# Retention with 128 rows for the sample's operands, and one block of modulation loads for each group

## The chip, the cores and the metric

The kernel runs on one core of a Trainium2 chip. The metric is the device time of one execution in microseconds (us), and what is compared is the median of several runs. Five engines run side by side, each in its own order: TensorE (PE in the profile, its weight loads PEld), VectorE (DVE), ScalarE (ACT), GpSimd (POOL) and SyncE (SP), which here issues most DMAs. They wait for each other by semaphores.

## What is computed

One layer of a streaming encoder, for 256 prompt rows and 32 sample rows together (T = 288), with 2048 features. Both kinds of rows use the same weights. Cut to what matters here:

```python
mod = silu(c) @ ada_w + ada_b                      # c: one vector for prompt, one for samples
shift, scale, gate = split(mod, 3)
h = rms_norm(x, g_pre) * (1 + scale) + shift
b, cg, u, zc, q, k, v, zr, ma, mb = split(h @ w_in)
y_conv = b * causal_conv(cg * u) * silu(zc)
# 8 heads of retention, q and k rotated by position, 128 wide, v 256 wide
scores = (q @ k.T) * decay                         # within a block
o = scores @ v + q_dec * (q @ state)
new_state = blk_dec * state + (k * k_dec).T @ v
y_ret = head_rms(o) * silu(zr)
merged = sigmoid(ma) * (y_conv @ w_branch[0]) + sigmoid(mb) * (y_ret @ w_branch[1])
x = x + gate * rms_norm(merged @ w_out, g_post)
```

Results are the new rows and the new states of the convolution and of retention.

## The kernel before

Activations lie with features in the partitions and the 288 rows in the free dimension. Every projection is made with three matmuls for each 128 x 128 piece of weights: the weights are cut into a high part (ScalarE, `whi`, L126 and L282) and a low part (VectorE, `wlo`, L127 and L289), the activations too (`hh`, `hl`), and high x high, high x low and low x high are added up in PSUM. Each of these is a matmul with 128 rows, 128 columns of weights and 288 moving columns.

*The start (L223 to L464)* runs in an order written out by hand for TensorE, ScalarE, VectorE and SP. The features are taken in eight groups of two 128-row tiles. For each group, shift and scale come from four loads of the modulation weights: `modulate` (L296) takes one load with eight small matmuls (L306), which write strips of 32 partitions; after the fourth, `gather_mod` (L313, L316), `factors` and `new_h` make the group's new activations. Then `multiply` (L357) multiplies three weight tiles of the group (w0, w1, w2: q, k and half of v), 48 matmuls each (L374, L375, L378), into `firsts`. VectorE or ScalarE adds the sums (L381, L383). While a tile is multiplied, later tiles are cut; `usual` and `rare` (L355) say after which quarter. In most groups a cut runs a tile and a half ahead of its use. The list `loads` (L250 to L254) sets both the order in which SP fetches and the order in which TensorE takes the loads. SP keeps eight loads in front (L459), in nine buffers, and issues one when the buffer it goes into is free. With m0 to m3 for the four loads of the next group's modulation, the order was w0 m0 m1 w1 m2 m3 w2 in group 0, and m0 w0 m1 w1 m2 m3 w2 in groups 1 to 6. Group 7 has no such loads.

*Retention (L473 to L621)* is ordered by a scheduler. For each pair of heads q and k are rotated (L481), for each head the gate is projected (L512) and, from head 4 on, the values (L503). A generator, `attend` (L520), is run a step at a time beside these projections: `step` (L169) is called after every twelve matmuls of the projection. Its steps, divided by `yield`, were: the keys turned (L532), scaled and cut; the values turned (L545, L546) and cut; the scores of two prompt blocks and of the samples (L553, L554, L555), decayed and cut; the new states (L572 for the samples); the outputs (L582 to L586), their norm; and three steps later the outputs turned back (L604). Products of two cut operands are three matmuls each (`add_product`, L497, L499 to L501). The prompt's operands have 128 rows; the samples' were sliced to 32: 32 rows of `kd` and `v`, of `pr` and `v`, of `on`; the samples' scores had 32 columns of k as weights. The operands' tiles were taken new by each head.

*After that* come the projections of the branches and of the convolution, and *the output projection (L757 on)*, whose result is copied (L773) and turned in 128 x 128 pieces (L775) and 128 x 32 pieces (L776).

Of the kernel before, what the change touches and what calls it, by code (L numbers as in the profile page):

```python
# [10 lines left out]
F32 = mybir.dt.float32  # L11
F32R = mybir.dt.float32r
# [4 lines left out]
P = 128  # L17
# [89 lines left out]
def hybrid_step(ctx: ExitStack, tc, x_prompt, x_sample, c_prompt, c_sample, state_conv, state_ret,  # L107
# [115 lines left out]
    with ExitStack() as phase:  # L223
# [27 lines left out]
        for g in range(NG):  # L251
            m = [(True, g + 1, s) for s in range(NK // MOD)] if g + 1 < NG else []
            w = [(False, g, u) for u in range(NU)]
            loads += (w[:1] + m[:1] if g == 0 else m[:1] + w[:1]) + m[1:2] + w[1:2] + m[2:] + w[2:]  # L254
        raws, parts_of, mod_ps, state_of = {}, {}, {}, {}
# [217 lines left out]
    with tc.tile_pool(name="ret", bufs=2, reuse_waits="tile") as rp:  # L473
# [5 lines left out]
        A.dma_start(out=qdec, in_=qdec_t)  # L479

        def rotate(ps, out):  # L481
# [12 lines left out]
        def parts(shape, name):  # L494
            return [rp.tile(shape, F32R, name=name + p, bufs=PB[name]) for p in ("h", "l")]

# [23 lines left out]
        def attend(h, q, k, vt, zs):  # L520

            state = rp.tile([P, DV], F32, name="state", bufs=1)
            A.dma_start(out=state, in_=state_ret[0, 0, h])
# [6 lines left out]
            for g in range(3):  # L530
                n = rows_of[g]
                nc.tensor.transpose(out=pk[:n, g * P:(g + 1) * P], in_=k[:, g * P:g * P + n], identity=ident)  # L532
            kd = parts([P, 3, DK], "kd")
            for g in range(3):
# [4 lines left out]
                                       op0=ALU.mult, op1=ALU.subtract)  # L539
            yield  # L540

            va, vb = aux_tile(), aux_tile()
            for f in range(2):
                for g in range(2):
                    nc.tensor.transpose(out=va[:, g * DV + f * P:g * DV + (f + 1) * P], in_=vt[f][:, g * P:(g + 1) * P], identity=ident)  # L545
                nc.tensor.transpose(out=vb[:TS, f * P:(f + 1) * P], in_=vt[f][:, TP:T], identity=ident)  # L546
            v = parts([P, 3, DV], "v")
            split(va.rearrange("p (g e) -> p g e", g=2), v[0][:, 0:2, :], v[1][:, 0:2, :])
# [5 lines left out]
            nc.tensor.matmul(psc[:, TP:TP + P], k[:, P:TP], q[:, P:TP], start=True, stop=True)  # L554
            nc.tensor.matmul(psc[:TS, TP + P:DC], k[:, TP:T], q[:, TP:T], start=True, stop=True)  # L555
# [3 lines left out]
            pr2 = parts([P, DC], "pr")  # L559
            split(pr[:, :TP + P], pr2[0][:, :TP + P], pr2[1][:, :TP + P])  # L560
# [4 lines left out]
            split(qs, *qs2)  # L565
            yield

            every, few = slice(None), slice(0, TS)
            pst = aux_tile()
            for g in range(2):  # L570
                add_product(pst[:, 0:DV], kd, v, (every, g), (every, g), g == 0, g == 1)
            add_product(pst[:, DV:2 * DV], kd, v, (few, 2), (few, 2), True, True)  # L572
            ns = rp.tile([P, 2, DV], F32, name="ns", bufs=1)
# [11 lines left out]
            add_product(ps[:TS, 0:DV], qs2, state2, (every,), (every,), True, False)  # L585
            add_product(ps[:TS, 0:DV], pr2, v, (few, slice(TP + P, DC)), (few, 2), False, True)  # L586
            so = rp.tile([P, 3], F32, name="so")
            V.memset(so, 1.0)
            on = rp.tile([P, 3, DV], F32, name="on", bufs=1)
            src = (po[:, 0:DV], po[:, DV:2 * DV], ps[:TS, 0:DV])  # L590
# [9 lines left out]
            for f in range(2):  # L600
                py = aux_tile()
                for g in range(3):
                    n = rows_of[g]
                    nc.tensor.transpose(out=py[:, g * P:g * P + n], in_=on[:n, g, f * P:(f + 1) * P], identity=ident[:n, :n])  # L604
                y = rp.tile([P, T], F32, name="y")
# [3 lines left out]
        for hp in range(NH // 2):  # L609
            qr, kr = turned(0, hp), turned(1, hp)  # L610
            for f in range(2):
                h = 2 * hp + f
                v = values(h)
                zs = gates(h)
                while len(side) > 1:
                    step()
                side.append(attend(h, qr[f], kr[f], v, zs))

# [138 lines left out]
    with tc.tile_pool(name="fin", bufs=2, reuse_waits="tile") as fp:  # L757
# [74 lines left out]
```

## Time and profile before

| what | value |
|---|---|
| median of three runs | 1369.86 us (1369.41 to 1370.79) |
| the profiled execution's own time | 1370.98 us |
| span of its records, first to last instruction | 1369.2 us |
| mean granted TensorE clock | 0.994 |
| TensorE busy | 1342.6 us (98%) |
| VectorE busy | 841.7 us (61%) |
| ScalarE busy | 552.2 us (40%) |
| read from HBM, mean rate over the span | 261.75 MB, 194 GB/s |

The start lasts to about 217 us, retention from there to about 440 us, the output projection begins at about 1247 us. In a timeline's row stand the start in us, the length, the engine, the line and operation, what is written and read, the form of the weights (rows*columns) and of the result and operand (partitions x elements), the number of records merged, and in brackets the idle time before and what ended it. A matmul's length is modelled and overlaps the next; the distance of two starts tells what it takes.

### The profile page before, as it was taken

How to read it: one execution, taken by the hardware profiler on the slowest of the kernel's cores; microseconds unless marked ns; L12 is line 12 of the kernel's file. 1: busy time of each engine (PE TensorE's matmuls, PEld its weight loads, DVE VectorE, ACT ScalarE, POOL GpSimd, SP SyncE). 2: the span in 40 equal slices, each digit the busy share in tenths (PEclk: the TensorE clock that was granted, in tenths of full speed). 3: DMA queues.
4: the chain of work that ended last, by engine and by line, in shares of the span. 5: the costliest groups of instructions: out<-in, count | busy, mean ns of one | idle time of the engine just before them, and what ended most of it. 6: DMA issues, size and time to landing. Idle time of an engine off the chain costs nothing.

```text
span 1369.2 us, 24142 instructions
## 1 busy us (share of the span) xinstructions
PE 1342.6 (98%) x10250; PEld 1306.0 (95%) x10250; DVE 841.7 (61%) x1398; ACT 552.2 (40%) x820; POOL 10.0 (1%) x18
## 2 busy tenths in 40 slices
PE   6999999999999999999999999999999999999996
PEld 5889899999999999999999999999999999999995
DVE  4567679865556666657676867765555334555443
ACT  4443346654444333333334333333333334334441
POOL 0000000000000000000000000000000000000000
PEclk9999999999999999999999999999999999999998
DMA  9988745444444666566566556664544545547531
GB/s 382 420 313 321 309 157 163 130 158 141 150 159 143 221 210 193 194 214 193 185 209 199 192 193 205 206 216 156 180 157 162 175 154 158 181 155 246 157 97 69
DMA packets 209092, 267.80 MB, mean 196 GB/s; under 512 B 5060, under 2 KB 199924, under 8 KB 201844
## 3 DMA queue, kind: packets, MB, share of 16 engines
q1 hardware_dynamic: 202784, 256.13, 55.2%
q10 hardware_dynamic: 6200, 10.13, 2.6%
q8 instruction: 80, 1.31, 0.4%
q14 instruction: 28, 0.23, 0.0%
HBM read 261.75 MB, written 4.49 MB: 194 GB/s over the span
## 4 chain that ended last, share of the span: by engine, by line
issue 68%; PE 30%; DVE 1%; DMA 0%; ACT 0%; POOL 0%; DVEq 0%; POOLq 0%; ACTq 0%
PE acc L161 4%; PE pair L374 4%; PE acc L162 4%; PE acc L164 4%; PE pair L378 4%; PE pair L375 4%; PE small L306 2%; PE aux L499 1%; PE aux L500 1%; PE aux L501 1%; PE aux L604 0%; PE pair L422 0%; DVE wlo L289 0%; DVE x L798 0%; DMA raw<-in_x_sample_dram 0%
## 5 line engine op out<-in xcount | busy, mean ns | idle before, releaser
L127 DVE TENSOR_TENSOR wlo<-raw,whi 128x1024 fp32r<-128x1024 f32 x336 | 411.2, 1224 | 347.8 <-ACT whi L126 347.0
L126 ACT CAST whi<-raw 128x1024 fp32r<-128x1024 f32 x336 | 352.7, 1050 | 516.0 <-PE acc L162 485.9
L161 PE MATMUL acc<-hh,whi 128*128 128x288 f32 x1920 | 531.6, 299 | 1.0 <-DVE firsts L383 1.0
L162 PE MATMUL acc<-hl,whi 128*128 128x288 f32 x1920 | 530.6, 297 | 0.0
L161 PEld LDWEIGHTS acc<-hh,whi 128*128 128x128 f32 x1920 | 360.9, 188 | 5.1 <-issue 1.7
L162 PEld LDWEIGHTS acc<-hl,whi 128*128 128x128 f32 x1920 | 361.2, 188 | 0.3
L164 PE MATMUL acc<-hh,wlo 128*128 128x288 f32 x1920 | 329.9, 294 | 0.0
L164 PEld LDWEIGHTS acc<-hh,wlo 128*128 128x128 f32 x1920 | 283.3, 188 | 0.0
L374 PE MATMUL pair<-hh,whi 128*128 128x288 f32 x384 | 111.5, 305 | 1.7 <-ACT hh L346 1.7
L643 DVE SCALAR_TENSOR_TENSOR gbc<-raw,sc,gbc 128x256 f32<-128x256 f32 x240 | 100.7, 484 | 14.5 <-DMA raw<-in_ada_w_dram 14.4
L375 PE MATMUL pair<-hl,whi 128*128 128x288 f32 x384 | 109.0, 299 | 0.1
L383 DVE TENSOR_TENSOR firsts<-pair,firsts 128x576 f32<-128x576 f32 x84 | 62.8, 755 | 40.7 <-PE pair L378 40.4
L378 PE MATMUL pair<-hh,wlo 128*128 128x288 f32 x384 | 84.0, 299 | 1.6 <-DVE wlo L289 1.6
L374 PEld LDWEIGHTS pair<-hh,whi 128*128 128x128 f32 x384 | 73.4, 191 | 10.3 <-ACT whi L282 4.8
L375 PEld LDWEIGHTS pair<-hl,whi 128*128 128x128 f32 x384 | 73.4, 191 | 0.3 <-DVE hl L352 0.3
L162 PE MATMUL acc<-ml,whi 128*128 128x288 f32 x256 | 70.7, 297 | 0.0
L161 PE MATMUL acc<-mh,whi 128*128 128x288 f32 x256 | 70.4, 297 | 0.0
L161 PE MATMUL acc<-ch,whi 128*128 128x288 f32 x256 | 70.0, 296 | 0.0
L161 PE MATMUL acc<-yh,whi 128*128 128x288 f32 x256 | 69.9, 296 | 0.0
L162 PE MATMUL acc<-yl,whi 128*128 128x288 f32 x256 | 69.8, 295 | 0.0
L162 PE MATMUL acc<-cl,whi 128*128 128x288 f32 x256 | 69.5, 294 | 0.0
L378 PEld LDWEIGHTS pair<-hh,wlo 128*128 128x128 f32 x384 | 62.9, 191 | 2.5 <-DVE wlo L289 2.3
(180 smaller groups left out, 1326.6 us busy)
## 6 DMA issues: line engine op xcount, KB each, us to landing
raw<-in_w_in_dram SPq DMA_DIRECT2D x120, 1024.0 KB, 5.0
raw<-in_w_branch_dram SPq DMA_DIRECT2D x32, 1024.0 KB, 5.5
raw<-in_ada_first_dram SPq DMA_DIRECT2D x28, 1024.0 KB, 6.9
raw<-in_w_first_dram SPq DMA_DIRECT2D x23, 1024.0 KB, 8.6
raw<-in_ada_w_dram SPq DMA_DIRECT2D x16, 1024.0 KB, 5.1
raw<-in_w_out_dram SPq DMA_DIRECT2D x16, 1024.0 KB, 5.4
raw<-in_ada_first_dram SPq DMA_DIRECT2D x8, 512.0 KB, 10.2
raw<-in_x_prompt_dram SPq DMA_DIRECT2D x2, 1024.0 KB, 5.7
```

The lines of the kernel that those rows point to most:

```text
L126: A.copy(out=hi, in_=src)
L127: V.tensor_tensor(out=lo, in0=src, in1=hi.bitcast(F32), op=ALU.subtract)
L161: nc.tensor.matmul(ps, hi[:, k, fs], xh[:, k0 + k, :], start=first and k == 0, stop=False)
L162: nc.tensor.matmul(ps, hi[:, k, fs], xl[:, k0 + k, :], start=False, stop=False)
L164: nc.tensor.matmul(ps, lo[:, k, fs], xh[:, k0 + k, :], start=False, stop=last and k == n - 1)
L306: nc.tensor.matmul(pm[at:at + 32, :GS * P], cs[:, kt, :], v[:, k, s, :], start=kt < 2, stop=kt >= NK - 2, tile_position=(0, at))
L374: nc.tensor.matmul(ps, hi[:, fs], hh[:, kt, :], start=k == 0, stop=False)
L375: nc.tensor.matmul(ps, hi[:, fs], hl[:, kt, :], start=False, stop=False)
L378: nc.tensor.matmul(ps, lo[:, fs], hh[:, kt, :], start=False, stop=k == GS - 1)
L383: V.tensor_tensor(out=sums, in0=pp[:, :, :T], in1=sums, op=ALU.add)
L499: nc.tensor.matmul(ps, a[0][ai], b[0][bi], start=first, stop=False)
L643: V.scalar_tensor_tensor(out=ga[:, b], in0=raw[:, k], scalar=sc[:, kt, b:b + 1], in1=ga[:, b], op0=ALU.mult, op1=ALU.add)
```

## The change

The lines of the diff are cut; `...` marks what is left out. In the rows below, line numbers of the changed code are its own.

```diff
-            loads += (w[:1] + m[:1] if g == 0 else m[:1] + w[:1]) + m[1:2] + w[1:2] + m[2:] + w[2:]
+            loads += w[:2] + m + w[2:]
...
+        v, kd, pr2 = parts([P, 3, DV], "v"), parts([P, 3, DK], "kd"), parts([P, DC], "pr")
+        on = rp.tile([P, 3, DV], F32, name="on", bufs=1)
+        for t in v + kd:
+            V.memset(t[:, 2, :].bitcast(F32), 0.0)
+        for t in pr2:
+            V.memset(t[:, TP + P:].bitcast(F32), 0.0)
+        V.memset(on[:, 2, :], 0.0)
...
+            keys = firsts.rearrange("p k t -> p (k t)")[:, (NF + h) * T:(NF + h) * T + TP + P]
...
-            kd = parts([P, 3, DK], "kd")
...
-            yield
...
-            v = parts([P, 3, DV], "v")
...
-            nc.tensor.matmul(psc[:TS, TP + P:DC], k[:, TP:T], q[:, TP:T], start=True, stop=True)
+            nc.tensor.matmul(psc[:, TP + P:DC], keys[:, TP:TP + P], q[:, TP:T], start=True, stop=True)
...
             yield
+            yield
...
-            add_product(pst[:, DV:2 * DV], kd, v, (few, 2), (few, 2), True, True)
+            add_product(pst[:, DV:2 * DV], kd, v, (every, 2), (every, 2), True, True)
...
-            add_product(ps[:TS, 0:DV], pr2, v, (few, slice(TP + P, DC)), (few, 2), False, True)
+            add_product(ps[:TS, 0:DV], pr2, v, (every, slice(TP + P, DC)), (every, 2), False, True)
...
-                    n = rows_of[g]
-                    nc.tensor.transpose(out=py[:, g * P:g * P + n], in_=on[:n, g, f * P:(f + 1) * P], identity=ident[:n, :n])
+                    nc.tensor.transpose(out=py[:, g * P:(g + 1) * P], in_=on[:, g, f * P:(f + 1) * P], identity=ident)
...
+            os = []
             for f in range(2):
                 o = fp.tile([P, T], F32, name="of")
                 A.copy(out=o, in_=pm[f][:, :T])
+                os.append(o)
+            for f, o in enumerate(os):
                 for g in range(2):
                     nc.tensor.transpose(out=pa[:, g * WC + f * P:g * WC + (f + 1) * P], in_=o[:, g * P:(g + 1) * P], identity=ident)
+            for f, o in enumerate(os):
                 nc.tensor.transpose(out=pb[:TS, f * P:(f + 1) * P], in_=o[:, TP:T], identity=ident)
```

The operands of retention are now made once and shared by the heads; the rows past the 32nd of the samples' part are set to zero once, and matmuls and transposes take all 128 rows. The samples' scores take 128 columns of keys, the 96 behind a head's own being the next tile of `firsts`; only 32 rows of the result are read. The turning of the values goes into the step of the keys, and an empty step stands behind the scores. In the start the order is w0 w1 m0 m1 m2 m3 w2 in every group. In the output projection both copies are made first, then the full transposes, then the narrow ones.

TensorE in the start, group 0, from the end of w1's multiplication to the first matmuls of w2. Before:

```order
L374 MATMUL pair<-hh,whi 128x288
L375 MATMUL pair<-hl,whi 128x288
L378 MATMUL pair<-hh,wlo 128x288 x2
L306 MATMUL small<-raw,cs 32x256 x16
L374 MATMUL pair<-hh,whi 128x288
L375 MATMUL pair<-hl,whi 128x288
```

The same place in the change:

```order
L374 MATMUL pair<-hh,whi 128x288
L375 MATMUL pair<-hl,whi 128x288
L378 MATMUL pair<-hh,wlo 128x288 x2
L306 MATMUL small<-raw,cs 32x256 x32
L374 MATMUL pair<-hh,whi 128x288
L375 MATMUL pair<-hl,whi 128x288
```

The two loads that stood between w0 and w1 have joined the two that stood here; w0 and w1 follow each other without a break.

TensorE in retention, head 0, where the outputs are turned back. Before:

```order
L164 MATMUL acc<-hh,wlo 128x288 x4
L604 MATMUL aux<-ident,on 128x128 x2
L604 MATMUL aux<-ident,on 128x32
L604 MATMUL aux<-ident,on 128x128 x2
L604 MATMUL aux<-ident,on 128x32
L161 MATMUL acc<-hh,whi 128x288
L162 MATMUL acc<-hl,whi 128x288
```

In the change:

```order
L162 MATMUL acc<-hl,whi 128x288
L164 MATMUL acc<-hh,wlo 128x288 x4
L610 MATMUL aux<-ident,on 128x128 x6
L161 MATMUL acc<-hh,whi 128x288
L162 MATMUL acc<-hl,whi 128x288
```

Six equal transposes stand where two of 32 rows stood among four of 128.

TensorE in the output projection, the end of the first 256 columns and the beginning of the next (the second piece is turned some matmuls later than the first). Before:

```order
L775 MATMUL aux<-ident,of 128x128 x2
L776 MATMUL aux<-ident,of 32x128
L161 MATMUL acc<-mh,whi 128x288
L162 MATMUL acc<-ml,whi 128x288
...
L161 MATMUL acc<-mh,whi 128x288
L775 MATMUL aux<-ident,of 128x128 x2
L776 MATMUL aux<-ident,of 32x128
L162 MATMUL acc<-ml,whi 128x288
```

In the change:

```order
L784 MATMUL aux<-ident,of 128x128 x2
L786 MATMUL aux<-ident,of 32x128
L161 MATMUL acc<-mh,whi 128x288
L162 MATMUL acc<-ml,whi 128x288
...
L161 MATMUL acc<-mh,whi 128x288
L784 MATMUL aux<-ident,of 128x128 x2
L786 MATMUL aux<-ident,of 32x128
L162 MATMUL acc<-ml,whi 128x288
```

The scheduler has put the transposes in the same order as before; nothing moved.

More of the change, by code (lines that the diff above doesn't have):

```diff
@@ L479, in hybrid_step, with parts @@
         A.dma_start(out=qdec, in_=qdec_t)
+        def parts(shape, name):
+            return [rp.tile(shape, F32R, name=name + p, bufs=PB[name]) for p in ("h", "l")]
+        v, kd, pr2 = parts([P, 3, DV], "v"), parts([P, 3, DK], "kd"), parts([P, DC], "pr")
[5 more added lines that the diff above has]
+        V.memset(on[:, 2, :], 0.0)
         def rotate(ps, out):
@@ L492, in turned @@
             return [rotate(s, s) for s in (firsts[:, NF * c + 2 * hp + f, :] for f in range(2))]
-        def parts(shape, name):
-            return [rp.tile(shape, F32R, name=name + p, bufs=PB[name]) for p in ("h", "l")]
         def add_product(ps, a, b, ai, bi, first, last):
@@ L558, in attend @@
             V.tensor_tensor(out=pr[:TS, TP + P:], in0=psc[:TS, TP + P:DC], in1=dec[:TS, TP + P:], op=ALU.mult)
-            pr2 = parts([P, DC], "pr")
             split(pr[:, :TP + P], pr2[0][:, :TP + P], pr2[1][:, :TP + P])
@@ L566, in attend @@
             yield
-            every, few = slice(None), slice(0, TS)
+            yield
+            every = slice(None)
             pst = aux_tile()
@@ L585, in attend @@
             add_product(ps[:TS, 0:DV], qs2, state2, (every,), (every,), True, False)
-            add_product(ps[:TS, 0:DV], pr2, v, (few, slice(TP + P, DC)), (few, 2), False, True)
+            add_product(ps[:TS, 0:DV], pr2, v, (every, slice(TP + P, DC)), (every, 2), False, True)
             so = rp.tile([P, 3], F32, name="so")
             V.memset(so, 1.0)
-            on = rp.tile([P, 3, DV], F32, name="on", bufs=1)
             src = (po[:, 0:DV], po[:, DV:2 * DV], ps[:TS, 0:DV])
@@ L612, in hybrid_step @@
                 h = 2 * hp + f
-                v = values(h)
+                vt = values(h)
                 zs = gates(h)
@@ L616, in hybrid_step @@
                     step()
-                side.append(attend(h, qr[f], kr[f], v, zs))
+                side.append(attend(h, qr[f], kr[f], vt, zs))
         beside = product(w_in[0], O_MB, hh, hl)
```

## The prediction

> **What bounds the kernel now.** I read the page first, then the table of windows, then TensorE's timeline at the places that the change touches, and last VectorE's timeline there.
>
> ```profile
> PE 1342.6 (98%) x10250; PEld 1306.0 (95%) x10250; DVE 841.7 (61%) x1398; ACT 552.2 (40%) x820; POOL 10.0 (1%) x18
> 200.00:300.00 100.00, 99.04 (x726) 94.11 (x726) 83.29 (x177) 58.80 (x127) 2.56 (x3) 1.00 0.48 153
> ```
>
> The first row is the page's busy time by engine: TensorE is busy for 98% of the span, VectorE (DVE) for 61%. The second is the window of 100 us with the end of the start and the first three heads of retention: TensorE 99.04 us, its weight loads 94.11, VectorE 83.29, ScalarE 58.80, granted clock 1.00. Nothing but TensorE's own order sets the time there, so an interval taken out between two matmuls comes off the end, unless a split or a copy falls behind. What matters is therefore not how long a matmul is (0.29 us, overlapped with its neighbours) but how far apart two starts are. That is read from the timeline.
>
> ```profile
> 239.58 0.28 PE L501 MATMUL aux<-vh,kdl 128*128 128x256 f32 x1
> 239.78 0.38 PE L499 MATMUL aux<-vh,kdh 32*128 32x256 f32 x1
> 240.01 0.28 PE L500 MATMUL aux<-vl,kdh 32*128 32x256 f32 x1
> 240.12 0.27 PE L501 MATMUL aux<-vh,kdl 32*128 32x256 f32 x1
> 240.33 0.40 PE L161 MATMUL acc<-hh,whi 128*128 128x288 f32 x1
> 240.57 0.29 PE L162 MATMUL acc<-hl,whi 128*128 128x288 f32 x1
> 240.70 0.30 PE L161 MATMUL acc<-hh,whi 128*128 128x288 f32 x1
> ```
>
> This is the end of the state product of head 0. Between like neighbours the starts are 0.11 to 0.12 us apart (240.01 to 240.12) for 256 columns, and 0.13 (240.57 to 240.70) for 288. Where rows change from 128 to 32 it is 0.20 and then 0.23; going back, 0.21 and 0.24. So each way costs about 0.2 us of TensorE's time, and no wait is recorded for it: the profile counts it as busy.
>
> **The change part by part.** The sum is made against the profiled execution, 1370.98 us with a span of 1369.2; the median of the three runs is 1369.86, so I take the difference off that.
>
> State product (L572). From 239.58 to 240.57 there are 0.99 us; four steps at 0.12 and one at 0.13 are 0.61. Padding to 128 rows saves 0.38 per head.
>
> ```profile
> 242.98 0.28 PE L501 MATMUL aux<-vh,prl 128*128 128x256 f32 x1
> 243.10 0.28 PE L499 MATMUL aux<-stateh,qsh 128*32 128x256 f32 x1
> ...
> 243.33 0.28 PE L501 MATMUL aux<-stateh,qsl 128*32 128x256 f32 x1
> ...
> 244.24 0.30 PE L162 MATMUL acc<-hl,whi 128*128 128x288 f32 x1
> ```
>
> Output product (L586). From 243.33, the last with 128 rows, over the three of 32 rows to the second matmul of the projection, 0.91 us; again 0.61 without the changes of rows: 0.30 per head. Its results stay 32 wide. That this costs nothing on the way in is in the first two rows (0.12). The way out of 32 columns at 128 rows is not shown for this kind; from nothing to the 0.2 that leaving 32 rows costs, and I take nothing, the value of the way in.
>
> ```profile
> 236.36 0.59 PE L553 MATMUL aux<-firsts 128*128 128x256 f32 x2
> 236.79 0.38 PE L554 MATMUL aux<-firsts 128*128 128x128 f32 x2
> 237.10 0.25 PE L555 MATMUL aux<-firsts 128*32 128x32 f32 x2
> 237.28 0.40 PE L161 MATMUL acc<-hh,whi 128*128 128x288 f32 x1
> 237.52 0.29 PE L162 MATMUL acc<-hl,whi 128*128 128x288 f32 x1
> ```
>
> ```profile
> 47.98 0.50 PE L316 MATMUL small<-pick,modrow 128*128 128x4 f32 x4
> 48.34 0.38 PE L374 MATMUL pair<-hh,whi 128*128 128x288 f32 x1
> 48.56 0.29 PE L375 MATMUL pair<-hl,whi 128*128 128x288 f32 x1
> ```
>
> Scores (L555). Here the rows are 128 already, and 32 columns of plain fp32 pay: 236.36 to 237.52 is 1.16 us. The nearest rows with 128 columns and a narrow moving operand are L316: 0.58 us for four passes and one step of 0.13, so 0.11 a pass. New: 0.43 (L553, unchanged), four passes at 0.11, 0.13: 1.00. Saved 0.16; between nothing (the wider load eats it) and 0.25 (the passes cost no more than now). The Trainium skill, page "TensorE: Matmul & The Clock Gate", section LDWEIGHTS, says that a weight load takes time by its columns, P / 1.2 ns. By that the two loads would go from 27 to 107 ns each and the scores would get 0.16 us longer a head; the sum would be 10.3 us, and the time 1359.6. The rows speak against it: from 236.79 to 237.52 the four narrow passes and one step take 0.73 us, where four of full width and one step make 0.57.
>
> Turning the outputs (L604).
>
> ```profile
> 248.89 1.10 PE L604 MATMUL aux<-ident,on 128*128 128x128 f32 x6
> 249.92 0.40 PE L161 MATMUL acc<-hh,whi 128*128 128x288 f32 x1
> 250.16 0.29 PE L162 MATMUL acc<-hl,whi 128*128 128x288 f32 x1
> ```
>
> ```profile
> 251.62 0.49 PE L532 MATMUL aux<-ident,firsts 128*128 128x128 f32 x3
> 251.86 0.38 PE L161 MATMUL acc<-hh,whi 128*128 128x288 f32 x1
> 252.08 0.29 PE L162 MATMUL acc<-hl,whi 128*128 128x288 f32 x1
> ```
>
> Six transposes, two of 32 rows: 1.27 us to the second matmul. The three of L532 never change rows and take 0.46, that is 0.11 each and 0.13. Six of that kind: 0.79. Saved 0.48.
>
> The keys' and the values' transposes standing together save nothing: these rows show that leaving them costs nothing. Per head 0.38 + 0.30 + 0.16 + 0.48 = 1.32 us, times 8: **10.6 us**.
>
> Start (L254). Each group's four modulation loads stood in two or three blocks; the order shows one. Group 0 loses one block, groups 1 to 6 two each: 13.
>
> ```profile
> 35.00 0.43 PE L378 MATMUL pair<-hh,wlo 128*128 128x288 f32 x2
> 35.35 1.93 PE L306 MATMUL small<-raw,cs 128*32 128x256 f32 x32
> 37.22 0.40 PE L374 MATMUL pair<-hh,whi 128*128 128x288 f32 x1
> ```
>
> ```profile
> 52.93 0.43 PE L378 MATMUL pair<-hh,wlo 128*128 128x288 f32 x2
> 53.28 1.07 PE L306 MATMUL small<-raw,cs 128*32 128x256 f32 x16
> 54.28 0.40 PE L374 MATMUL pair<-hh,whi 128*128 128x288 f32 x1
> 54.52 0.29 PE L375 MATMUL pair<-hl,whi 128*128 128x288 f32 x1
> ```
>
> Each matmul of L306 leaves two records. Sixteen more cost 0.87 us (35.35 to 37.22 against 53.28 to 54.28). A block of sixteen takes, from 53.19 (52.93 and two steps) to 54.39 (54.52 less a step), 1.20; 0.33 of it is the way in and out. 13 times that is 4.3 us.
>
> But a block also gave ScalarE and VectorE time to cut the next weights.
>
> ```profile
> 35.50 1.23 DVE L289 TENSOR_TENSOR wlo<-raw,whi 128x1024 fp32r<-128x1024 f32 x1 [1.81 <-ACT whi L282]
> 52.71 2.35 DVE L289 TENSOR_TENSOR wlo<-raw,whi 128x1024 fp32r<-128x1024 f32 x2
> ```
>
> After 35.13 the second weight tile would now start at 35.26 and need its second low part five steps on, at 35.9; VectorE ends it at 36.73: 0.8 us of wait. The first tile of group 1 would start at 53.19 and need its low part at 53.85; VectorE ends at 55.06: 1.2. In later groups the cut runs a tile and a half ahead (L355), and the last group, which has no such block, lies in the window above but for its first microseconds, and TensorE idles for less than 1 us there; I take nothing, and 0.3 a group as the bound (1.5). Start: 4.3 - 2.0 = **2.3 us**. The four loads of a block free their buffers within 4 us, so their followers queue together on SP's queue; they are wanted a whole group later, the weights among them a tile and a half later.
>
> The zeroing, 1088 columns on VectorE once, stands before the last sums of the start. I have no row of that shape and put it at no more than the 1.23 us of one 1024-wide split; it is hidden, since the splits run ahead of TensorE, and costs 1.2 if they don't.
>
> Output projection (L775, L776). The copies stand ahead in the code, but the order is the same as before: three transposes, projection, three transposes. Nothing.
>
> Sum: 10.6 + 2.3 = 12.9; 1369.86 - 12.9 = **1357.0 us**.
>
> **The rivals.**
>
> *VectorE takes over in the early heads.* The window holds some three heads, so about 4 us of it go, and 83.29 us of VectorE would stand in 96: 87%. If the first four heads wait for their splits, 4 times 1.32 and the zeroing are lost: 1363.5. Against it: TensorE idles less than 1 us of the window as it is. If it happened in all eight heads, 10.6 us would go and 1367.6 be left, no change that can be told. The later heads, with projections between, speak against this.
>
> *The start gives it all back.* With no pause between tiles, every group waits the 0.8 to 1.2 us that I charge to two places: five more groups, 5 us, 1362.0. Against it: the last group, above.
>
> *The padded loads come into the open, and it gets slower.*
>
> ```profile
> L162 PEld LDWEIGHTS acc<-hl,whi 128*128 128x128 f32 x1920 | 361.2, 188 | 0.3
> ```
>
> A full load takes 188 ns. If loads were hidden only beside a matmul with other rows, the eight padded ones of each head (three, three and two) would lose their cover: 8 x 8 x 0.19 = 12 us, and no change of rows would be saved: 1369.9 + 12 - 2.3 = 1379.6. It ends slower as soon as more than 2.3 us of loads lie bare. The Trainium skill states this rule ("TensorE: Matmul & The Clock Gate", Part 3, what overlaps): loads overlap with matmuls in flight only when the row group differs. The trace says the reverse: full loads of 188 ns follow full matmuls at 0.13 us a step, and it is where rows differ that steps grow to 0.2.
>
> *Columns set the price, not rows.* Then leaving the output product still costs 0.2 us a head: 1358.6, inside the forecast's range.
>
> **How the numbers follow.** Forecast 0.86; VectorE in four heads 0.05, in all 0.03; the start 0.04; slower 0.02. For the range, below: no wait at the start (-2.0), the scores at their best (-0.7), and the scatter of the runs, 1354.0. Above: 1.6 for columns, 1.5 for later groups, 1.2 for the zeroing or as much for the scores, 1361.3. The rivals outside hold 0.14. A difference under 0.2% (2.7 us) can't be told from none: faster 0.95, same 0.03, slower 0.02.
>
> **What would show it.** In the timeline after: steps of 0.12 through the nine matmuls of the state product and 0.13 behind them; six transposes and the return in 0.8 us; seven blocks of 64 records of L306, with the ways in and out as now; a wait for a low part at about 35.3 and 53.2 us. The window of the first heads keeps TensorE at 99%. Wrong would be: steps of 0.2 still at those places, waits of TensorE for VectorE beyond the two, or a start that ends no earlier than now.

## The result and the profile after

| | before | changed |
|---|---|---|
| median | 1369.69 us (1369.41 to 1370.79, 4 runs) | 1357.57 us (1357.26 to 1357.92, 4 runs) |
| the profiled execution | 1370.98 us, span 1369.2 | 1357.76 us, span 1356.0 |
| granted clock, mean | 0.994 | 0.994 |
| first matmul of retention (first L161) | 217.49 us | 214.65 us |
| from there to the first matmul of the gates (L651, in the changed kernel L657) | 283.10 us | 273.06 us |
| from there to the last matmul | 855.37 us | 855.03 us |

The ratio is 0.9907, with a 95% interval of 0.9895 to 0.992: 12.1 us less, where 12.9 were predicted. The table puts 2.8 us of the 13.2 between the two profiled executions into the start, 10.0 into retention and 0.3 into everything behind it. What the tables call retention ends with the first matmul of the gates, 63.6 us behind the last transposes of the outputs in both kernels; these 63.6 us are projections and did not change. One of the later executions of the kernel before took 7424 us and is left out of every comparison.

Busy time by engine of the changed kernel, from its page, and the window of its first heads:

```profile
PE 1327.6 (98%) x10250; PEld 1305.6 (96%) x10250; DVE 840.0 (62%) x1405; ACT 551.5 (41%) x820; POOL 10.0 (1%) x18
200.00:300.00 100.00, 98.40 (x759) 97.38 (x758) 84.29 (x189) 61.72 (x138) 3.41 (x4) 1.00 0.51 159
214.65:487.71 273.06, 272.40 (x2089) 271.00 (x2089) 187.09 (x364) 138.74 (x276) 6.80 (x8) 1.00 0.53 168
```

The same stage of the kernel before, from its table of windows:

```profile
217.49:500.59 283.10, 283.10 (x2088) 271.92 (x2089) 186.99 (x361) 139.73 (x276) 6.80 (x8) 1.00 0.50 159
```

The stage has the same work in less time: 2088 matmuls start in it in both kernels (the 2089th record of the changed one is the gates' first matmul), with 187 us of VectorE. TensorE was called busy for all of 283.10 us before, and its busy time falls by 10.7. That is how a price looks that no wait records. In return 0.66 us of the stage (273.06 less 272.40) are now idle, and the window of the first heads stands at 98.4%, not at the 99% that was predicted.

The four places of retention in the changed kernel, head 0, in TensorE's timeline. First the end of the state product:

```profile
236.16 0.28 PE L510 MATMUL aux<-vh,kdl 128*128 128x256 f32 x1
236.28 0.28 PE L508 MATMUL aux<-vh,kdh 128*128 128x256 f32 x1
236.40 0.28 PE L509 MATMUL aux<-vl,kdh 128*128 128x256 f32 x1
236.52 0.28 PE L510 MATMUL aux<-vh,kdl 128*128 128x256 f32 x1
236.63 0.29 PE L161 MATMUL acc<-hh,whi 128*128 128x288 f32 x1
236.76 0.29 PE L162 MATMUL acc<-hl,whi 128*128 128x288 f32 x1
```

Steps of 0.12 throughout and 0.13 behind: 0.60 us from 236.16 to 236.76, where it was 0.99. Then the end of the output product:

```profile
239.18 0.28 PE L510 MATMUL aux<-vh,prl 128*128 128x256 f32 x1
...
239.54 0.28 PE L510 MATMUL aux<-stateh,qsl 128*32 128x256 f32 x1
...
239.89 0.28 PE L510 MATMUL aux<-vh,prl 128*32 128x256 f32 x1
240.01 0.29 PE L161 MATMUL acc<-hh,whi 128*128 128x288 f32 x1
240.14 0.29 PE L162 MATMUL acc<-hl,whi 128*128 128x288 f32 x1
```

0.60 us from 239.54 to 240.14, where it was 0.91; the step out of 32 columns (239.89 to 240.01) is 0.12. Then the scores, and the turning of the outputs:

```profile
231.53 0.59 PE L561 MATMUL aux<-firsts 128*128 128x256 f32 x2
231.96 0.39 PE L562 MATMUL aux<-firsts 128*128 128x128 f32 x2
232.18 0.31 PE L563 MATMUL aux<-firsts 128*128 128x32 f32 x2
232.32 0.38 PE L161 MATMUL acc<-hh,whi 128*128 128x288 f32 x1
232.54 0.29 PE L162 MATMUL acc<-hl,whi 128*128 128x288 f32 x1
```

```profile
244.81 0.82 PE L610 MATMUL aux<-ident,on 128*128 128x128 f32 x6
245.38 0.38 PE L161 MATMUL acc<-hh,whi 128*128 128x288 f32 x1
245.60 0.29 PE L162 MATMUL acc<-hl,whi 128*128 128x288 f32 x1
```

1.01 us (was 1.16) and 0.79 us (was 1.27). In the mean of the eight heads, each from the first matmul of the place to the second of the projection behind it, the four places went from 1.584, 2.207, 1.162 and 1.266 us to 1.196, 1.904, 1.011 and 0.789: saved 0.388, 0.303, 0.151 and 0.477.

The start, TensorE's timeline. First the wait in the tile ahead of group 0's one block, then that block, then the waits in the first tile of group 1:

```profile
36.98 0.40 PE L378 MATMUL pair<-hh,wlo 128*128 128x288 f32 x1 [0.60 <-DVE wlo L289]
...
42.85 3.66 PE L306 MATMUL small<-raw,cs 128*32 128x256 f32 x64
46.44 0.40 PE L374 MATMUL pair<-hh,whi 128*128 128x288 f32 x1
```

```profile
54.00 0.40 PE L374 MATMUL pair<-hh,whi 128*128 128x288 f32 x1 [0.15 <-ACT whi L282]
...
55.28 0.40 PE L378 MATMUL pair<-hh,wlo 128*128 128x288 f32 x1 [0.62 <-DVE wlo L289]
```

Seven such blocks of 64 records stand where there were twenty. Both predicted waits are there. They end at 36.98 and 55.28 us, where the prediction had VectorE end its cuts at 36.73 and 55.06; the 35.3 and 53.2 of its last paragraph are the starts of the two tiles. What made the first one late is read from the chain of waits:

```profile
34.08 0.64 ACT firsts L381
34.73 0.96 ACT whi L282
35.70 1.24 DVE wlo L289
36.98 0.40 PE pair L378
```

ScalarE copies the last sums first, then cuts the high part, VectorE waits for that and makes the low part, TensorE waits for that. And something is gone that the kernel before had, in its timeline:

```profile
46.93 0.40 PE L378 MATMUL pair<-hh,wlo 128*128 128x288 f32 x1 [0.39 <-DVE wlo L289]
```

New and not predicted is a wait at head 1. TensorE, where the samples' values are turned, and then VectorE and ScalarE ahead of it:

```profile
248.42 0.28 PE L555 MATMUL aux<-ident,firsts 128*32 128x128 f32 x1 [0.66 <-DVE y L612]
```

```profile
243.11 0.43 DVE L127 TENSOR_TENSOR statel<-state,stateh 128x256 fp32r<-128x256 f32 x1 [1.83 <-ACT stateh L126]
...
247.91 0.82 DVE L612 TENSOR_TENSOR y<-aux,zs 128x288 f32<-128x288 f32 x2
```

```profile
242.67 0.41 ACT L126 CAST stateh<-state 128x256 fp32r<-128x256 f32 x1 [1.84 <-DMA state<-in_state_ret_dram]
```

Read backwards: L555 writes a PSUM bank from which VectorE has yet to read the first head's outputs (L612). VectorE comes to that late, since it stood 1.83 us for ScalarE, and ScalarE stood 1.84 us for the second head's state, whose load goes into the one buffer that the first head's state leaves.

### The profile page after: what moved, and what is told of

Read it like the earlier page. It is cut to its first block, busy times and chain, and to the rows that moved or that the text cites. A ratio compares the mean times of both kernels' runs of the same rounds, so it can differ in the third digit from the quotient of the medians.

```text
span 1356.0 us, 24148 instructions
## 1 busy us (share of the span) xinstructions
PE 1327.6 (98%) x10250; PEld 1305.6 (96%) x10250; DVE 840.0 (62%) x1405; ACT 551.5 (41%) x820; POOL 10.0 (1%) x18
## 4 chain that ended last, share of the span: by engine, by line
issue 68%; PE 28%; DVE 2%; ACT 1%; DMA 1%; POOL 0%; DVEq 0%; POOLq 0%; ACTq 0%
PE acc L161 4%; PE pair L374 4%; PE pair L378 4%; PE acc L162 4%; PE acc L164 4%; PE pair L375 4%; PE small L306 2%; PE aux L508 0%; PE aux L509 0%; PE aux L510 0%; DVE wlo L289 0%; PE pair L422 0%; DMA state<-in_state_ret_dram 0%; PE aux L610 0%; DMA raw<-in_x_sample_dram 0%
## 5 line engine op out<-in xcount | busy, mean ns | idle before, releaser
L161 PE MATMUL acc<-hh,whi 128*128 128x288 f32 x1920 | 528.6, 297 | 0.9 <-DVE firsts L383 0.9
L161 PEld LDWEIGHTS acc<-hh,whi 128*128 128x128 f32 x1920 | 361.0, 188 | 1.7 <-ACT whi L126 1.1
L374 PE MATMUL pair<-hh,whi 128*128 128x288 f32 x384 | 110.2, 301 | 1.9 <-ACT hh L346 1.7
L374 PEld LDWEIGHTS pair<-hh,whi 128*128 128x128 f32 x384 | 73.4, 191 | 5.4 <-issue 2.9
L161 PE MATMUL acc<-mh,whi 128*128 128x288 f32 x256 | 70.2, 296 | 0.0
L161 PE MATMUL acc<-ch,whi 128*128 128x288 f32 x256 | 70.0, 296 | 0.0
L161 PE MATMUL acc<-yh,whi 128*128 128x288 f32 x256 | 69.9, 296 | 0.0
```

The source lines that it names most:

```text
L161: nc.tensor.matmul(ps, hi[:, k, fs], xh[:, k0 + k, :], start=first and k == 0, stop=False)
L374: nc.tensor.matmul(ps, hi[:, fs], hh[:, kt, :], start=k == 0, stop=False)
```

## Experiments

Start and retention are read from each trace, as in the table above. "Start, full clock" is the time from the first matmul of the start's multiplication (L374) to the first of retention, with 0.108 us taken off for each step of 0.24 us in place of 0.13 among its first matmuls; there were 12 to 26 of these, and the last section shows why they must come off.

| kernel | median us (runs) | start, full clock | retention |
|---|---|---|---|
| before | 1369.69 (4) | 191.1 | 283.10 |
| changed | 1357.57 (4) | 188.1 | 273.06 |
| changed, run again | 1356.84 (4) | 188.1 | 273.01 |
| start alone | 1366.94 (9) | 188.1 | 282.85 |
| retention alone | 1360.00 (5) | 191.0 | 273.21 |
| old steps | 1356.42 (4) | 188.1 | 272.00 |
| narrow scores | 1357.15 (4) | 188.1 | 273.27 |
| 64 rows | 1365.97 (7) | 188.0 | 281.51 |
| grouped transposes, in the kernel before | 1367.27 (11) | 190.9 | 280.35 |
| earlier cuts | 1355.77 (4) | 185.8 | 273.19 |
| two states | 1356.15 (4) | 188.2 | 272.39 |
| earlier cuts and two states | 1354.18 (4) | 185.8 | 272.24 |
| earlier cuts and old steps | 1354.09 (4) | 185.7 | 272.01 |
| wide moving operand | 1358.59 (1) | 188.1 | 274.95 |

"Retention" is the time from the first matmul of retention to the first matmul of the gates. The kernel before, run beside the experiments, had medians of 1370.2, 1370.05 and 1369.81 us.

**Are the two parts independent?** The kernel before with the new loads, and the changed kernel with the old ones:

```diff
-            loads += (w[:1] + m[:1] if g == 0 else m[:1] + w[:1]) + m[1:2] + w[1:2] + m[2:] + w[2:]
+            loads += w[:2] + m + w[2:]
```

```diff
-            loads += w[:2] + m + w[2:]
+            loads += (w[:1] + m[:1] if g == 0 else m[:1] + w[:1]) + m[1:2] + w[1:2] + m[2:] + w[2:]
```

> The kernel before with the new order of the loads alone; retention as it was. Theory (the start pays for each 64-record block: 13 fewer at 0.33 us, less two waits for w1's low parts): the start ends 2.8 us earlier, as in the changed kernel, and that carries through: 1369.7 - 2.8 = 1366.9 us. Rival (what the start gains is given back at the first heads, where work of VectorE is due): no change, 1369.4 to 1370.0 us. Rival (the retention's edits and the start's help each other, since VectorE's rotations of the heads come out of the same queue): 1368 us or more, and the two alone do not add up to the 12.1 us of both.

> The changed kernel with the old order of the loads: only the retention's edits are left. Theory (1.32 us a head for changes of rows that are gone, less one wait of 0.7 us for VectorE at the second head): 1369.7 - 10.0 = 1359.7 us, between 1359.2 and 1360.3. Rival (the wait at the second head grows or goes with the start, since VectorE then stands elsewhere in its queue): outside of that by 0.7 us. Rival (VectorE limits the heads when the start ends late): above 1361 us. If both parts are independent, the gains of this kernel and of the one with the loads alone add up to 12.1 us within 0.5.

Measured: 1366.94 us (1366.34 to 1367.37) and 1360.00 us (1359.47 to 1360.67), ratios to the kernel before 0.9975 (0.9965 to 0.9985) and 0.9924 (0.9912 to 0.9937). In the traces the first has 3.0 us less of start and retention as before, the second the start of before and 9.9 us less of retention. By stage the parts add up: start and retention each keep their gain when the other is undone (3.0 and 9.9, with 3.0 and 10.0 for both together), and the wait at head 1 is there without the new start too (0.6 us). The medians are less exact: against the kernel before that ran beside them the two gained 3.3 and 10.2 us, 13.5 together, where 12.1 within 0.5 was expected; both edits together gained 12.1 in one comparison and 13.0 in another. The rivals of a mutual effect fall by the stages.

**Does any change of rows pay, or only few rows, or bare loads?** The changed kernel with 64 rows where it has 128:

```diff
-            add_product(pst[:, DV:2 * DV], kd, v, (every, 2), (every, 2), True, True)
+            add_product(pst[:, DV:2 * DV], kd, v, (half, 2), (half, 2), True, True)
...
-            add_product(ps[:TS, 0:DV], pr2, v, (every, slice(TP + P, DC)), (every, 2), False, True)
+            add_product(ps[:TS, 0:DV], pr2, v, (half, slice(TP + P, DC)), (half, 2), False, True)
...
+                    n = P if g < 2 else 64
```

> The changed kernel with the samples' operands cut to 64 rows in the state product, the output product and the transposes of the outputs; their zero rows past the 64th are left out of the products, and the result is the same. Theory A (any number of rows under 128 is a change of the array's shape and pays for it both ways, whatever it moves): state 0.38, output 0.30 and transposes 0.48 us a head come back, 1.16 x 8 = 9.3, so 1357.6 + 9.3 = 1366.9 us. Rival B (the price goes by the rows left out): a good half of that, some 1363 us. Rival C (by the Trainium skill's page TensorE: Matmul & The Clock Gate, part 3 on what overlaps, loads to another row group overlap and full ones do not; then 64 rows would be no worse than 128): 1357.6 us or less.

Measured: 1365.97 us (1365.26 to 1366.63). The state product of head 0 in that kernel's timeline:

```profile
235.82 0.28 PE L510 MATMUL aux<-vh,kdl 128*128 128x256 f32 x1
236.03 0.38 PE L508 MATMUL aux<-vh,kdh 64*128 64x256 f32 x1
236.25 0.28 PE L509 MATMUL aux<-vl,kdh 64*128 64x256 f32 x1
236.37 0.28 PE L510 MATMUL aux<-vh,kdl 64*128 64x256 f32 x1
236.57 0.40 PE L161 MATMUL acc<-hh,whi 128*128 128x288 f32 x1
236.81 0.29 PE L162 MATMUL acc<-hl,whi 128*128 128x288 f32 x1
```

0.99 us from 235.82 to 236.81, as with 32 rows. All three places return: state 0.39, output 0.30, transposes 0.53 us a head, 9.8 us in all; the wait at head 1 is absent in this run, which takes off 0.8, and the plain steps of the projections vary by half a microsecond. Theory A holds, B and C fall. Why a change pays is seen in TensorE's weight loads at that place, first with 64 rows, then with 128 in the changed kernel:

```profile
236.02 0.18 PEld L508 LDWEIGHTS aux<-vh,kdh 64*128 64x128 f32 x1
```

```profile
236.28 0.19 PEld L509 LDWEIGHTS aux<-vl,kdh 128*128 128x128 f32 x1
```

The load of L508's 64 rows begins at 236.02, together with its own matmul (236.03). The load of L509 with 128 rows begins at 236.28, when the matmul ahead of it begins, 0.12 us before its own (236.40). Equal shapes load ahead; a new number of rows does not. In the eight heads of this kernel, and of the kernel before, 64 loads stand at a change of rows, into 64 or 32 or back to 128, and each begins within 3 ns of its own matmul. The Trainium skill, page "TensorE: Matmul & The Clock Gate", Part 3 (what overlaps), says that a load overlaps with matmuls in flight only when the row group differs. Here it is the other way round, by 1.2 us a head.

**Per change, or per small instruction?** The kernel before, with its transposes of outputs in another order:

```diff
-            for f in range(2):
-                py = aux_tile()
-                for g in range(3):
...
+            for gs in ((0, 1), (2,)):
+                for f, py in enumerate(pys):
+                    for g in gs:
```

> The kernel before with its six transposes of the outputs in another order: the four of 128 rows first, then the two of 32, so that there is one change to 32 rows and one back a head where there were two of each. Nothing else is changed. Theory A (the price is paid for each change of shape): half of 0.48 us a head goes, 0.24 x 8 = 1.9, so 1369.7 - 1.9 = 1367.8 us, and the block takes 1.03 us a head where it took 1.27. Rival B (each 32-row instruction is slow by itself): no change, 1369.7 us, block 1.27. Rival C (the second bank is taken earlier, and VectorE's work on the first begins later, so that the end of the block delays VectorE): slower than 1369.7 us.

Measured: 1367.27 us (1366.85 to 1368.12), ratio 0.9979 (0.997 to 0.9988). The place in its timeline:

```profile
247.91 0.84 PE L605 MATMUL aux<-ident,on 128*128 128x128 f32 x6
248.68 0.40 PE L161 MATMUL acc<-hh,whi 128*128 128x288 f32 x1
248.91 0.29 PE L162 MATMUL acc<-hl,whi 128*128 128x288 f32 x1
```

1.00 us where it was 1.27: 0.26 us a head, a little over half of 0.48. The same six transposes with half the changes cost half the price, so it is paid per change: rival B falls. No padding is needed for this half. The whole stage got 2.75 us shorter; 2.1 of it are these blocks, the rest is in the plain steps of the projections, whose sum differs by some tenths of a microsecond from kernel to kernel.

**The scores.** The changed kernel with 32 columns of keys again:

```diff
-            nc.tensor.matmul(psc[:, TP + P:DC], keys[:, TP:TP + P], q[:, TP:T], start=True, stop=True)
+            nc.tensor.matmul(psc[:TS, TP + P:DC], k[:, TP:T], q[:, TP:T], start=True, stop=True)
```

> The changed kernel with the samples' scores loaded from 32 columns again instead of 128; all else as changed. Theory of the prediction (a load of 32 columns costs the change of the array's shape, 0.15 us a head between the scores' first and last matmul): 1357.6 + 8 x 0.15 = 1358.8 us, and the scores take 1.16 us a head again. By the rule of the Trainium skill's page TensorE: Matmul & The Clock Gate, section LDWEIGHTS, that a load's price goes by its columns, it would be some 1.3 us less than now, 1356.3 us; that is an estimate. Rival (the price of the scores in the kernel before came from what stood ahead of them, the values' transposes of 32 columns, and not from their own load): no change, 1357.6 us.

Measured: 1357.15 us (1357.09 to 1358.04), no slower. Read by the time alone, the term would be refuted. The place in its timeline says otherwise:

```profile
231.43 0.25 PE L563 MATMUL aux<-firsts 128*32 128x32 f32 x2
231.61 0.40 PE L161 MATMUL acc<-hh,whi 128*128 128x288 f32 x1
231.85 0.29 PE L162 MATMUL acc<-hl,whi 128*128 128x288 f32 x1
```

The scores take 1.164 us a head again, 0.153 more, 1.2 us in all. Against that, the wait at head 1 is gone in this run (0.8 us), the plain steps came out 0.2 lower, and retention began 0.8 us earlier. ScalarE waits 1.0 us for the state, not 1.8: head 0 is 0.15 us longer, but the larger part is that ScalarE goes on 3.8 us after the load's issue where it was 4.5, and why is not shown. Of the earlier beginning, 0.6 us are an earlier first matmul of the start (23.25 us, not 23.87), the rest has the reason given in the last section. The groups of weight loads of this line, first here, then in the changed kernel:

```profile
L563 PEld LDWEIGHTS aux<-firsts 128*32 128x32 f32 x16 | 1.1, 108 | 1.0
```

```profile
L563 PEld LDWEIGHTS aux<-firsts 128*128 128x128 f32 x16 | 2.4, 192 | 0.0
```

The narrow load is shorter, 108 ns against 192. The Trainium skill's page "TensorE: Matmul & The Clock Gate", section LDWEIGHTS, gives P / 1.2 ns for P columns, an estimate of 27 and 107 ns: the trace agrees on the difference (84 ns, where that makes 80), while each load is some 80 ns longer than the page's figure. The place was dearer all the same: the loads' row sat idle for 1.0 us in all before the narrow loads, and for nothing before the wide ones. The first narrow load begins at 231.43 us, with its own matmul; in the changed kernel the wide one begins at 232.07, 0.11 us ahead of its own (232.18). That is the sign seen above where the number of rows changes. Is it the narrow load, or its short multiplication? The same kernel, with 128 moving columns:

```diff
+            nc.tensor.matmul(psc[:TS, TP + P:DC + 96], k[:, TP:T], q[:, T - P:T], start=True, stop=True)
```

> The changed kernel with the samples' scores loaded from 32 columns, as in the kernel before, but multiplied with 128 columns of the queries in place of 32 (96 of them unused prompts' columns, whose results are left out). Theory D (a load of 32 columns costs the change by itself): the last two products of the scores come after a step of 0.20 us again, and the first product behind them has a second step of 0.24 us. Theory E (it costs only with a short multiplication behind it, since the transposes of 32 columns and the output product of 32 columns, with 128 and 256 moving, show no such step): steps of 0.11 us throughout and 0.216 us behind, as with 128 columns. Two passes of 128 columns take 0.16 us a head more than two of 32 in either case, 1.3 us in all, so its time is read from these steps and not from the sum: D 1358 to 1360, E 1358 to 1359.5 us.

Measured: 1358.59 us, one run. Steps into, between and out of the two passes in the mean of the heads: 0.205, 0.133 and 0.203 us, and 0.239 behind. Theory D holds: this load pays by itself. It does not follow that columns set the price, since the output product (32 columns of rounded operands, 0.12) and the transposes of 32 columns (0.11) pay nothing. What distinguishes these three kinds stays open.

**The wait at head 1.** Two ways to remove it: the values turned in a step of their own, as before, or two buffers for the state.

```diff
+            yield
+
             va, vb = aux_tile(), aux_tile()
...
             yield
-            yield
```

```diff
-            state = rp.tile([P, DV], F32, name="state", bufs=1)
+            state = rp.tile([P, DV], F32, name="state", bufs=2)
```

> The changed kernel with the values' transposes back in a step of their own and the empty step behind the scores gone, as in the kernel before; the operands keep their 128 rows. Theory (the one wait of 0.66 us at the second head, where the samples' values take a bank that VectorE has not yet read for the first head's output, is there only because keys and values are transposed in one step): that wait goes, the keys' and values' transposes keep their mean elsewhere, 1357.6 - 0.7 = 1356.9 us. Rival (merging the two steps saved a turn between different operands in the other heads, which now comes back: 0.1 us or more a head): 1357.6 to 1358.5 us. Rival (VectorE's queue is what is late, and the wait only moves to the next user of its banks): 1357.6 us.

> The changed kernel with two buffers in place of one for the state that each head loads, so that the second head's load need not wait for the first head's last reading of it. Theory (the 0.7 us wait at the second head starts with that load: it is issued at 238.2 us, 0.5 us behind the first head's new state, lands 4.0 us later, ScalarE and then VectorE stand 1.8 us for it, and VectorE's reading of the first head's outputs is late by that much): the wait goes, 1357.6 - 0.8 = 1356.8 us, retention (from its first product to the first product behind it) takes 272.3 us where it took 273.1. Rival (VectorE is late by its own work, the rotations of later heads ahead of the outputs): the wait stays, 1357.6 us. Rival (the rows on ScalarE and VectorE come in another order and the wait moves elsewhere): 1357.3 to 1358 us.

Measured: 1356.42 us (1355.71 to 1356.58) and 1356.15 us (1356.07 to 1356.72); retention 272.00 and 272.39 us. In both the wait is gone. With two states ScalarE's row is this:

```profile
239.27 0.41 ACT L126 CAST stateh<-state 128x256 fp32r<-128x256 f32 x1
```

It waits for nothing, and neither does VectorE behind it. That confirms the chain read above: the load into the single buffer, not VectorE's own work, made it late. The old steps remove the wait too. There the load landed 2.5 us after its issue, while in the changed kernel ScalarE stood until 4.5 us after it (the 4.0 us of the expectation belong to the next head's load); the cause was not found. Apart from the wait, turning the keys and the values together costs or saves 0.1 us in eight heads. The stage is 0.2 to 0.4 us shorter with the old steps than with two states, in two traces of each; that lies in the plain steps of the projections and stays open.

**The waits of the start.** ScalarE's and VectorE's cuts come earlier: in the first tile a quarter of a tile earlier, in the second one after each of its last three quarters, where two had stood behind the last; the third and fourth tiles follow the usual order:

```diff
-        usual, rare = {1: 1, 3: 1}, {(0, 0): {1: 1, 2: 1}, (0, 1): {3: 2}, (0, 2): {1: 1, 2: 1}, (1, 0): {1: 1, 2: 1, 3: 1}}
+        usual, rare = {1: 1, 3: 1}, {(0, 0): {0: 1, 1: 1}, (0, 1): {1: 1, 2: 1, 3: 1}}
```

> The changed kernel with another share of the weights' splitting at the start: in the first two tiles of the start ScalarE takes more of the rounding of w1 and w2 (one line of numbers), the products are the same. Theory (VectorE's differences for the low parts are late in the first two tiles since each waits for ScalarE's rounded part: four waits, 2.5 us in all at 25, 27, 37 and 55 us): the waits at 37 and 55 us go, 1357.6 - 1.3 = 1356.3 us, and the first step of the keys, queries and values (line 161) begins at about 213.3 us. Rival (the low parts are late because VectorE's own time is used up, so that another order gives nothing): 1357.6 us. Rival (the high parts come later for it and TensorE waits there): above 1358 us.

Measured: 1355.77 us (1355.4 to 1355.82), first matmul of retention at 212.39. The row of the low parts in the list of who waited for whom, first of the changed kernel, then here:

```profile
PE pair L378 <- DVE wlo L289: 2.5, 4, 0.7
```

```profile
PE pair L378 <- DVE wlo L289: 1.2, 2, 0.7
```

The two waits at 37 and 55 us are gone, the two at 26 and 27 are left, and the start is 2.3 us shorter at full clock. VectorE had the time; the order of the cuts was the limit. Its wait at head 1 stayed (0.8 us).

**Together,** and the changed kernel once more beside them:

> The changed kernel once more, unchanged, beside the versions that are compared with it. Both theories expect 1357.6 us, between 1356.8 and 1358.4. Retention should take 273.1 us again, and the wait of 0.7 to 0.8 us at the second head's values should be there again (it was in three of the traces with this order of VectorE's and ScalarE's work, and not in the one in which the state's load was waited for by 0.8 us less). The time from the first product of the start to the first product of the queries should be 188.0 us once 0.11 us is taken off for each step at half clock (the traces so far agree on that to 0.2 us), whatever the number of such steps is.

> The changed kernel with both the earlier cuts of w1 and w2 and the two buffers for the state. Theory (two separate waits, one in the start and one at the second head): their gains add up, 2.1 and 0.7 us, 1357.6 - 2.8 = 1354.8 us; the start to the first product of the queries 185.9 us without its half-clock steps, retention 272.4 us. Rival (the earlier start meets VectorE's backlog at the first heads): 1355.8 us, as with the cuts alone.

> The changed kernel with the earlier cuts of w1 and w2 and with the values' transposes in a step of their own again, the state in one buffer. Theory (that step removes the same wait of the second head as the two buffers, by giving the state's load time, and 0.3 us beside): 1357.6 - 2.1 - 1.1 = 1354.4 us, retention 272.0 us. Rival (the wait left by chance, because the state's load landed 2.5 us after its issue in that run and 4.0 in the others): the wait is there again and retention takes 272.8 to 273.1 us, 1355.4 us.

Measured: 1356.84 us (1356.6 to 1357.12) for the changed kernel again, ratio 0.9905 (0.989 to 0.992); 1354.18 us (1353.33 to 1355.09) and 1354.09 us (1353.23 to 1354.47), ratios 0.9886 (0.987 to 0.9903) and 0.9884 (0.9869 to 0.9899). The gains add up: each is 2.7 us faster than the changed kernel that ran beside them, where 2.8 and 3.2 were expected from 1357.6; by stage the start keeps its 2.3, and retention 0.8 and 1.0. The rival that the old steps help by chance is not borne out: in this second trace the wait is absent again, and the load lands after 2.4 us again. Both versions beat both kernels by their medians.

## Why the prediction was right

*State product, 0.38 a head:* 0.388. *Output product, 0.30, with nothing for leaving 32 columns:* 0.303, and the step out is 0.12. The experiment with 64 rows gives both back. *Output transposes, 0.48:* 0.477; half the changes, half the price. *Scores, 0.16 by way of the narrow passes of L316:* 0.151, given back by the narrow load. Here the sum came out and its split did not: the prediction had four passes of 0.11 and a step of 0.13, the steps are 0.11, 0.11, 0.03, 0.11 and 0.22 us. *Keys and values together, nothing:* nothing by itself. The sum was 10.6 us; the four places give 1.319 x 8 = 10.55.

Retention gained 10.0 and not 10.55, because one wait was not in the sum: at head 1 the keys' and values' block is 0.8 us longer. That leaves 9.7; the other 0.3 is in the projections' plain steps, 0.2 ns each. The prediction counted a merged step only by its matmuls. It did not ask which banks that step takes and who must have read them first. Of the rival that VectorE takes over in the early heads this is one head out of four, for a reason that lay with a DMA.

*Start, 4.3 - 2.0 = 2.3:* 3.0 at full clock. Summed over all steps between two starts, the blocks of L306 with their ways in and out cost 4.4 us less than before, against 4.3. The waits were priced a little low: behind 33 us, steps above 0.16 us between the matmuls of the tiles hold 2.5 us more than plain steps (0.9 about 36.98, 1.5 in the tile at 54.00 to 62), against 0.8 + 1.2. The term that is off is one left out: the kernel before had 0.8 us of such steps itself, most of it the wait at 46.93, and they went. 4.4 - 2.5 + 0.8 is 2.7; the other 0.3 is in a thousand plain steps, 0.3 ns each. It is not scatter: they take 132.4 to 132.5 ns in the three traces with the old order of loads, and 132.1 to 132.2 in the others. Why is not shown. Later groups showed no wait, as taken. The earlier cuts leave 0.2 of the 2.5 us, hence their 2.3.

*Zeroing, hidden, at most 1.2:* the seven instructions took 1.3 us between 208 and 212 us, and TensorE waited for nothing from 56 to 214 us. Its wait at the start's end, for VectorE's last sum, is 0.94 us; it was 0.96 in the kernel before. *Output projection, nothing:* the 855 us behind the gates' first matmul moved by 0.3.

So 12.9 was predicted, and 12.1 and 13.0 were measured in two comparisons. The forecast's two errors, 0.7 too little for the start and 0.6 too much for retention, cancelled; that the total came so near is in this part luck.

## What to carry over

Where an engine is called busy all the time, read the distance of starts and not the length of rows: a load that cannot go ahead costs 0.12 to 0.2 us each way here and is recorded as work. Pad, or group by shape, what stands between large matmuls; then ask, for each step moved, which buffers it takes and who must be done with them. An edit of 1 us is judged by the stage that it touches, since the total may carry an unrelated wait of the same size.

## What the runs showed of the hardware

In the start TensorE is granted half its clock for a stretch, and how many matmuls that slows differs between runs of one program. The window of 30 to 32 us, of the changed kernel and of its second run (the last three columns are granted clock, DMA share and GB/s):

```profile
30.00:32.00 2.00, 2.00 (x11) 2.00 (x10) 0.03 (x1) 0.67 (x1) 0.00 (x0) 0.50 1.04 434
```

```profile
30.00:32.00 2.00, 2.00 (x15) 2.00 (x14) 0.28 (x1) 1.15 (x2) 0.00 (x0) 0.83 0.97 401
```

By the granted clock of narrower windows, the half clock lasts 6.8 us in both (3.4 in the kernel with grouped transposes), but from 26.2 to 33.0 us in the one and from 23.8 to 30.7 in the other. Up to 27.4 and 27.9 us TensorE is still held up by the first cuts, so the two stretches hold 25 and 12 slow steps: 1.4 us of difference, as much as several of the effects here. The Trainium skill, page "TensorE: Matmul & The Clock Gate", Part 1, says that the window in which TensorE's activity is watched runs freely, so that the number of slow matmuls varies from run to run; these traces agree (12 to 26). Without those steps the start of seven kernels with the new order of loads and the old cuts, eight traces in all, agrees within 0.2 us.

Also unexpected: 64 rows cost as much as 32, and half of the transposes' price goes without any padding.
